# Merging the small-product groups of a chunked gated recurrence: twelve groups a chunk become six, in shared PSUM banks

## The chip, the cores and the metric

The kernel runs on one core of a Trainium2 chip. The metric is the device time of one execution in microseconds (us). All arithmetic is fp32; the large products are made of three passes over split operands.

## The reference, cut to what matters

The program is a decoder layer: projections, a gated linear recurrence (HGRN2), sliding-window attention, two layer norms and a mixture of experts. The change touches the recurrence alone. For each of 4 heads, with keys, queries and decays of width 128, it computes scores that decay from token s to token t:

```python
b = jnp.cumsum(lb_c, axis=2)
diff = b[:, :, :, None, :] - b[:, :, None, :, :]
decay = jnp.exp(jnp.where(tri[:, :, None], diff, -jnp.inf))
scores = jnp.einsum('bhtk,bhtsk,bhsk->bhts', qb, decay, kb)
o_intra = jnp.einsum('bhts,bhsv->bhtv', scores, vb)
...
new_state = (jnp.exp(b_last[:, :, 0, :])[..., None] * state
             + jnp.einsum('bhsk,bhsv->bhkv', kb * jnp.exp(b_last - b), vb))
```

## The kernel before

The program runs in stages: projections with attention, projections with the recurrence, mixing and routing, and the experts. This text is about the second, the recurrence stage (`hgrn`, L520 to L684, and the stage's call at L1450 to L1453).

**The recurrence.** The 1024 tokens are handled as 8 chunks n of 128. For each chunk five tiles are loaded (`load`, L540: `hl` the log decays, `hk`, `hq`, `hv`, `hg`). The 128x128 score matrix of each head is not computed at once, since the decay between two tokens doesn't factor over a whole chunk. It is put together from a diagonal part (`diag`) and seven levels h = 1, 2, 4, ... 64 (`level`): at level h, each pair of neighbouring blocks of h tokens gives one block of scores, and for that level the decay factors over the reference token between the two blocks. `prep_level` (L563) makes the factors of a level in one tile `hE` (two exponentials on ACT at L573 and L576; on DVE a subtraction L575, two multiplications L577 and L580, and the addition L581 that turns `hl` into the running sum that the next level needs).

**The products of a level.** For the diagonal and the levels 1 to 16, `blocks` (L548) makes four products a head, one for each run of 32 tokens: 128 rows deep, 32 columns of weights, 32 moving columns, written to the 32x32 block on the diagonal of the head's 128x128 area in a PSUM bank (`pb`). Four heads make 16 products a group, each two passes in fp32, and the profile shows a pass as one matmul. Of each 32x32 block only the entries that belong to the level count, so `keep` (L535) copies them under a mask into the score tile `hst`, one DVE instruction for each run of 32 partitions. Level 32 makes 8 products (L591, L592), level 64 makes 4 of 64 columns (L589); ACT copies these (L596 to L599).

**The rest of a chunk.** `decay` transposes the decayed keys (L620) for the state; `output` (L643, L645) multiplies scores with values and queries with the last state; its result is squared on ACT (L647), summed on DVE (L649), turned into a norm on POOL (L690) and applied on DVE (L653); `state` (L629, L635) makes the new state; `out` transposes and stores the result (L414).

**The order.** The twelve groups of a chunk get due numbers (L659 to L672), and all groups are sorted by them. When group i is issued, the preparation of group i + 2 is issued first (`group`, L679). `weave` (L231) puts the groups into a stream of filler: the branch-gate projections, 768 matmuls of 512 columns (L103 to L105, three passes `xh*wh`, `xl*wh`, `xh*wl` for each product), spread evenly over the groups. PE issues in this written order; the other engines' instructions are ordered by a scheduler. Filler weights come in as `wr` (L187), and are split into `wh` on ACT (L98) and `wl` on DVE (L99). Filler results leave PSUM through ACT (L508) and DVE (L509).

**Buffers.** `hE` and the chunk's other tiles come out of one set of 24 SBUF tiles; weights, inputs and their splits come out of another set, `q4`, of 36 tiles of twice that size. The `pb` banks are 5, the filler's `mm` banks 3. The loads of the next stage (`mixing_start`) are put in as groups counted from the end (L1451).

Of the kernel before, what the change touches and what calls it, by code (L numbers as in the profile page):

```python
# [5 lines left out]
F32 = mybir.dt.float32  # L6
# [19 lines left out]
RUNS = [slice(b, b + 32) for b in range(0, 128, 32)]  # L26
LEVELS = (64, 32, 16, 8, 4, 2, 1)
# [34 lines left out]
class Builder:  # L62
# [457 lines left out]
    def hgrn(self):  # L520
# [3 lines left out]
        nc = self.nc  # L524
        mm = nc.tensor.matmul
        V = {}
# [4 lines left out]
        def mask(name):  # L531
            m = self.c("ident") if name == 0 else lev[:, WHERE[f"lev{name}"][0] - lo:WHERE[f"lev{name}"][1] - lo]
            return m.bitcast(I32)

        def keep(st, name, pp):  # L535
            for b in RUNS:
                m = mask(name)[b, b][:, None, :].to_broadcast([32, 4, 32])
                nc.vector.copy_predicated(st[b, :, b], m, pp[b, :, b])

        def load(n):  # L540
            t0 = slice(n * 128, n * 128 + 128)
            for nm, src in (("hl", self.hl[:, :, t0]), ("hk", self.hk[:, :, t0]), ("hq", self.hq[:, :, t0]),
                            ("hv", self.hv[t0].rearrange("p (h k) -> p h k", h=4)),
                            ("hg", self.hg[t0].rearrange("p (h k) -> p h k", h=4))):
                V[nm, n] = self.tile([128, 4, 128], F32, nm, 2)
                nc.sync.dma_start(V[nm, n], src)

        def blocks(out, l, r):  # L548

            for b in RUNS:  # L550
                mm(out[b, b], l[:, b], r[:, b], start=True, stop=True)

        def prep_diag(n):
            V["st", n] = self.tile([128, 4, 128], F32, "hst", 1)
            nc.gpsimd.memset(V["st", n], 0.0)

        def diag(n):
            pp = self.bank("pb", (128, 4, 128))
            for hd in range(4):
                blocks(pp[:, hd], V["hk", n][:, hd], V["hq", n][:, hd])  # L560
            keep(V["st", n], 0, pp)

        def prep_level(n, h):  # L563
            q, kT, b = V["hq", n], V["hk", n], V["hl", n]
            ns = 4 * (64 // h)

            def view(t):
                return t.rearrange("p h (s two x) -> p (h s) two x", two=2, x=h)

            e = self.tile([128, 4, 128], F32, "hE", 2)  # L570
            ev, bv, qv, kv = view(e), view(b), view(q), view(kT)
            ref = bv[:, :, 0, h - 1:h].to_broadcast([128, ns, h])
            nc.scalar.activation(ev[:, :, 1], bv[:, :, 1], AF.Exp)  # L573
            if h > 1:
                nc.vector.tensor_sub(ev[:, :, 0], ref, bv[:, :, 0])  # L575
                nc.scalar.activation(ev[:, :, 0], ev[:, :, 0], AF.Exp)  # L576
                nc.vector.tensor_mul(ev[:, :, 0], ev[:, :, 0], kv[:, :, 0])  # L577
            else:
                nc.gpsimd.tensor_copy(ev[:, :, 0], kv[:, :, 0])
            nc.vector.tensor_mul(ev[:, :, 1], ev[:, :, 1], qv[:, :, 1])  # L580
            nc.vector.tensor_add(bv[:, :, 1], bv[:, :, 1], ref)  # L581
            V["e", n, h] = e

        def level(n, h):
            e, st = V.pop(("e", n, h)), V["st", n]
            pp = self.bank("pb", (128, 4, 128))
            for hd in range(4):
                if h == 64:
                    mm(pp[0:64, hd, 64:128], e[:, hd, 0:64], e[:, hd, 64:128], start=True, stop=True)  # L589
                elif h == 32:  # L590
                    mm(pp[0:32, hd, 32:64], e[:, hd, 0:32], e[:, hd, 32:64], start=True, stop=True)  # L591
                    mm(pp[64:96, hd, 96:128], e[:, hd, 64:96], e[:, hd, 96:128], start=True, stop=True)  # L592
                else:
                    blocks(pp[:, hd], e[:, hd], e[:, hd])
            if h == 64:
                nc.scalar.copy(st[0:64, :, 64:128], pp[0:64, :, 64:128])  # L596
            elif h == 32:
                nc.scalar.copy(st[0:32, :, 32:64], pp[0:32, :, 32:64])
                nc.scalar.copy(st[64:96, :, 96:128], pp[64:96, :, 96:128])  # L599
            else:  # L600
                keep(st, h, pp)

        def prep_decay(n):
            b = V["hl", n]
            kdT = self.tile([128, 4, 128], F32, "hkT", 1)
            for hd in range(4):
                nc.scalar.activation(kdT[:, hd], b[:, hd], AF.Exp, scale=-1.0, bias=b[:, hd, 127:128])
            nc.vector.tensor_mul(kdT, kdT, V["hk", n])
            qb = self.tile([128, 4, 128], F32, "hqb", 1)
            nc.scalar.activation(qb, b, AF.Exp)  # L610
            ebl = self.tile([128, 4], F32, "hebl", 2)
            nc.gpsimd.tensor_copy(ebl, qb[:, :, 127])
            nc.vector.tensor_mul(qb, qb, V["hq", n])
            V["d", n] = kdT, qb, ebl

        def decay(n):
            kdT, _, _ = V["d", n]
            kp = self.bank("pb", (128, 4, 128))
            for hd in range(4):
                nc.tensor.transpose(kp[:, hd], kdT[:, hd], self.c("ident"))  # L620
            kd = self.tile([128, 4, 128], F32, "hkd", 1)
            nc.scalar.copy(kd, kp)
            V["kd", n] = kd
# [32 lines left out]
        def out(n):  # L656
            self.out_T(V.pop(("o", n)).rearrange("p h d -> p (h d)"), self.oad, n, "pb")

        none = lambda: None  # L659
        groups = []  # L660
        for n in range(8):
            at = 11 * n
            groups.append((at, lambda n=n: prep_diag(n), lambda n=n: diag(n)))
            for i, h in enumerate(reversed(LEVELS)):
                pre = lambda n=n, h=h: prep_level(n, h)
                if i == 3 and n < 7:
                    pre = lambda n=n, h=h: (load(n + 1), prep_level(n, h))
                groups.append((at + 1 + i, pre, lambda n=n, h=h: level(n, h)))
            groups.append((at + 8, lambda n=n: prep_decay(n), lambda n=n: decay(n)))
            groups.append((at + 10.5, none, lambda n=n: state(n)))  # L670
            groups.append((at + 9.6, none, lambda n=n: output(n)))
            groups.append((at + 13.5, none, lambda n=n: out(n)))  # L672
        groups.sort(key=lambda t: t[0])
        load(0)
        ahead = 2
# [758 lines left out]
    def build(self):  # L1434
        pool = self.tc.tile_pool
        with pool(name="base", bufs=1) as self.base, pool(name="dr", bufs=1, space=DRAM) as self.dr:
            self.setup()
            self.n2 = 13
            self.banks = {"mm": 3, "sc": 1, "pa": 3}
            with pool(name="sb1", bufs=1, reuse_waits="tile") as self.sb, \  # L1440
                    pool(name="ps1", bufs=1, space=PSUM, reuse_waits="tile") as self.ps, self.pe_order():
                self.att_proj()
                self.hg_consts()
                stream = self.stream()
                self.weave(self.attention(), stream, 164)
            self.n2 = 24
            self.banks = {"mm": 3, "pb": 5}
            with pool(name="sb2", bufs=1, reuse_waits="tile") as self.sb, \
                    pool(name="ps2", bufs=1, space=PSUM, reuse_waits="tile") as self.ps, self.pe_order():
                groups = self.hgrn()  # L1450
                for n, fn in zip((16, 11, 7), self.mixing_start()):  # L1451
                    groups.insert(len(groups) - n, fn)
                self.weave(groups, stream, 164, 8)  # L1453
            self.n2 = 4
            with pool(name="sb3", bufs=1, reuse_waits="tile") as self.sb:
                self.banks = {"mm": 4, "pa": 1, "tb": 1, "pb": 2}
                with pool(name="ps3", bufs=1, space=PSUM, reuse_waits="tile") as self.ps:
                    with self.all_order():
                        self.mixing()
                        self.slots()  # L1460
                    self.overflow()
                self.banks = {"mm": 4, "pb": 4}
                with pool(name="ps4", bufs=1, space=PSUM, reuse_waits="tile") as self.ps, self.all_order():
                    self.moe()
# [44 lines left out]
```

## Time and profile before

| | |
|---|---|
| runs of the kernel before, us | 1413.33, 1416.44, 2682.26 (median 1416.44) |
| the profiled execution, us | 1413.68 |
| its span, us | 1411.5 |
| mean granted TensorE clock | 0.985 |
| PE busy in the span | 1347.8 us (95%) |
| DVE busy | 1083.8 us (77%) |
| ACT busy | 790.0 us (56%) |
| recurrence stage | 297.5 to 546 us of the span |

The span is the time from the first to the last instruction in the trace; 2.2 us lie around it. Busy time of PE counts overlapping matmuls once, so what a group costs is read from the starts of the matmuls around it, not from its busy time. Rows name engine, source line, operation, output<-input, and the number of equal instructions.

### The profile page before, as it was taken

The page shows a single profiled execution, that of the slowest core. Times are in us where ns is not written, and L with a number is a line of the kernel's source. Part 1 is how long each engine was busy: PE and PEld are TensorE (multiplying, and loading weights), DVE is VectorE, ACT ScalarE, POOL GpSimd, SP SyncE. Part 2 cuts the span into 40 slices and gives each one's busy share as a digit, 9 for nine tenths or more (in the row PEclk, how much of TensorE's full clock was granted, in tenths as well). Part 3 has the DMA queues.
Part 4 walks back from the last instruction along what each step waited for, and adds up shares of the span by engine and source line. Part 5 has one row for each costly group of instructions (what it writes and reads, how often), then busy time and mean ns, then how long its engine had stood idle before and what let it go on. Part 6 is the DMA issues. An engine that isn't in the chain of part 4 may idle for free. (4 is left out here: it accounts for less than half of the span.)

```text
span 1411.5 us, 22907 instructions
## 1 busy us (share of the span) xinstructions
PE 1347.8 (95%) x8314; PEld 1099.6 (78%) x8314; DVE 1083.8 (77%) x1798; ACT 790.0 (56%) x1282; POOL 243.3 (17%) x160
## 2 busy tenths in 40 slices
PE   7999999999999999999998999999999999999844
PEld 5888899987777778788787788888888888888721
DVE  4268986878778885767746889999999999999645
ACT  4367545424444443312101888888888888888532
POOL 0001212210010001310001122222222222222123
PEclk9999999999999999999999999999999999999967
DMA  6124233253334234865538899999999999999962
GB/s 244 59 88 149 87 112 102 72 175 106 119 129 150 84 105 144 271 194 164 203 135 330 308 364 371 366 356 359 353 350 356 356 357 361 364 365 359 370 259 96
DMA packets 142564, 327.84 MB, mean 232 GB/s; under 512 B 18614, under 2 KB 59702, under 8 KB 142448
## 3 DMA queue, kind: packets, MB, share of 16 engines
q1 hardware_dynamic: 132800, 308.78, 60.3%
q0 software_dynamic: 9648, 17.57, 4.9%
q8 instruction: 66, 1.08, 0.3%
q14 instruction: 50, 0.41, 0.1%
HBM read 291.43 MB, written 52.43 MB: 244 GB/s over the span
## 5 line engine op out<-in xcount | busy, mean ns | idle before, releaser
L99 DVE TENSOR_TENSOR el<-er,eh 128x1024 fp32r<-128x1024 f32 x368 | 436.6, 1220 | 51.9 <-ACT eh L98 34.9
L98 ACT CAST eh<-er 128x1024 fp32r<-128x1024 f32 x368 | 368.7, 1052 | 99.1 <-PE mm L104 82.9
L103 PE MATMUL mm<-xh,wh 128*128 128x512 f32 x480 | 200.2, 417 | 7.8 <-ACT wh L98 6.8
L103 PE MATMUL mm<-eh,xh 128*128 128x512 f32 x496 | 196.4, 396 | 0.0
L104 PE MATMUL mm<-el,xh 128*128 128x512 f32 x496 | 196.2, 395 | 0.0
L105 PE MATMUL mm<-eh,xl 128*128 128x512 f32 x496 | 196.1, 395 | 0.0
L104 PE MATMUL mm<-xl,wh 128*128 128x512 f32 x480 | 189.6, 395 | 0.8 <-DVE xl L99 0.8
L105 PE MATMUL mm<-xh,wl 128*128 128x512 f32 x480 | 190.0, 396 | 0.0
L103 PEld LDWEIGHTS mm<-xh,wh 128*128 128x128 f32 x480 | 91.3, 190 | 26.0 <-ACT wh L98 6.8
L105 PEld LDWEIGHTS mm<-eh,xl 128*128 128x128 f32 x496 | 93.2, 188 | 22.6
L104 PEld LDWEIGHTS mm<-el,xh 128*128 128x128 f32 x496 | 93.2, 188 | 22.3
L103 PEld LDWEIGHTS mm<-eh,xh 128*128 128x128 f32 x496 | 93.2, 188 | 22.3
L105 PEld LDWEIGHTS mm<-xh,wl 128*128 128x128 f32 x480 | 91.2, 190 | 21.1 <-DVE wl L99 0.8
L1075 POOL DMA_INDIRECT xg<-x1d,gi x32 | 58.1, 1816 | 279.7 <-PE pb L1138 245.4
L104 PEld LDWEIGHTS mm<-xl,wh 128*128 128x128 f32 x480 | 91.5, 191 | 16.4 <-DVE xl L99 1.1
L103 PE MATMUL mm<-eh,hth 128*128 128x512 f32 x240 | 100.2, 418 | 0.0
L1079 POOL DMA_INDIRECT zd<-y,gi x29 | 70.4, 2429 | 156.9 <-ACT y L1229 156.9
L105 PE MATMUL mm<-eh,htl 128*128 128x512 f32 x240 | 94.8, 395 | 0.0
L104 PE MATMUL mm<-el,hth 128*128 128x512 f32 x240 | 94.8, 395 | 0.0
L103 PE MATMUL mm<-wh,xh 128*128 128x256 f32 x256 | 73.1, 285 | 0.0
L105 PE MATMUL mm<-wh,xl 128*128 128x256 f32 x256 | 72.4, 283 | 0.0
L104 PE MATMUL mm<-wl,xh 128*128 128x256 f32 x256 | 72.4, 283 | 0.0
(257 smaller groups left out, 2527.4 us busy)
## 6 DMA issues: line engine op xcount, KB each, us to landing
er<-w_g SPq DMA_DIRECT2D x128, 512.0 KB, 12.1
er<-w_u SPq DMA_DIRECT2D x128, 512.0 KB, 12.5
er<-w_d SPq DMA_DIRECT2D x128, 512.0 KB, 12.0
wr<-w_in SPq DMA_DIRECT2D x38, 512.0 KB, 3.8
gated<-st SPq DMA_DIRECT2D x32, 256.0 KB, 2.1
st<-gated SPq DMA_DIRECT2D x32, 256.0 KB, 3.3
xr<-xt SPq DMA_DIRECT2D x8, 512.0 KB, 9.1
wab<-w_a SPq DMA_DIRECT2D x16, 256.0 KB, 3.9
```

The lines of the kernel that those rows point to most:

```text
L98: self.nc.scalar.copy(hi, src)
L99: (eng or self.nc.vector).tensor_sub(lo, src, hi.bitcast(F32))
L103: mm(out, lh, rh, start=start, stop=False)
L104: mm(out, lh, rl, start=False, stop=False)
L105: mm(out, ll, rh, start=False, stop=stop)
L1075: self.nc.gpsimd.indirect_dma_start(to, None, rows, bass.IndirectOffsetOnAxis(ap=self.column(self.gi, e), axis=0), bounds_check=T - 1, oob ...
L1079: self.nc.gpsimd.indirect_dma_start(self.zd, bass.IndirectOffsetOnAxis(ap=idx, axis=0), y, None, bounds_check=T - 1, oob_is_err=False, com ...
```

## The change

The diagonal and the levels 1 and 2 become one group, the levels 4 and 8 another, 16 and 32 a third, 64 and the transposes of the decay a fourth, output and state a fifth; `out` stays alone. In a merged group all products are issued first, one level behind the other, and the copies out of PSUM (now returned as functions) behind all of them. The levels of one group share one bank: each 32x32 block is written at its rows' run shifted by 0, 1 or 2 runs of columns (`RUNS[(i + shift) % 4]`), and `keep` reads it from there. The number of products and of copies stays the same. The two levels' factors lie in one `q4` tile of two halves instead of two smaller tiles. The preparation still runs two groups ahead, and a group is now up to two levels. The due numbers and the places of the next stage's loads are rewritten to match.

```diff
-        def keep(st, name, pp):
-            for b in RUNS:
+        def keep(st, name, pp, shift):
+            for i, b in enumerate(RUNS):
                 m = mask(name)[b, b][:, None, :].to_broadcast([32, 4, 32])
-                nc.vector.copy_predicated(st[b, :, b], m, pp[b, :, b])
+                nc.vector.copy_predicated(st[b, :, b], m, pp[b, :, RUNS[(i + shift) % 4]])
...
-        def blocks(out, l, r):
-
-            for b in RUNS:
-                mm(out[b, b], l[:, b], r[:, b], start=True, stop=True)
+        def blocks(out, l, r, shift):
+
+            for i, b in enumerate(RUNS):
+                mm(out[b, RUNS[(i + shift) % 4]], l[:, b], r[:, b], start=True, stop=True)
...
-        def diag(n):
-            pp = self.bank("pb", (128, 4, 128))
+        def diag(n, pp):
             for hd in range(4):
-                blocks(pp[:, hd], V["hk", n][:, hd], V["hq", n][:, hd])
-            keep(V["st", n], 0, pp)
+                blocks(pp[:, hd], V["hk", n][:, hd], V["hq", n][:, hd], 2)
+            return lambda: keep(V["st", n], 0, pp, 2)
...
-            e = self.tile([128, 4, 128], F32, "hE", 2)
...
-                    blocks(pp[:, hd], e[:, hd], e[:, hd])
...
+                    blocks(pp[:, hd], e[:, hd], e[:, hd], shift)
+
+            def post():
...
+                    keep(st, h, pp, shift)
+
+            return post
+
+        def prep_levels(n, hs):
+            t = self.q4([128, 2, 512], F32, "hE")
+            es = [t[:, j].rearrange("p (h x) -> p h x", h=4) for j in range(2)]
+            for h, e in zip(hs, es):
+                prep_level(n, h, e)
+
+        def levels(n, hs):
+
+            pp = self.bank("pb", (128, 4, 128))
+            posts = [diag(n, pp)] if hs[0] == 1 else []
+            posts += [level(n, h, pp, j) for j, h in enumerate(hs)]
+            for post in posts:
+                post()
...
-            at = 11 * n
...
+            at = 4 * n
+            groups += [(at, lambda n=n: (prep_diag(n), prep_levels(n, (1, 2))), lambda n=n: levels(n, (1, 2))),
+                       (at + 1, lambda n=n: prep_levels(n, (4, 8)), lambda n=n: levels(n, (4, 8))),
+                       (at + 2, lambda n=n: (n < 7 and load(n + 1), prep_levels(n, (16, 32))), lambda n=n: levels(n, (16, 32))),
+                       (at + 3, lambda n=n: (prep_levels(n, (64,)), prep_decay(n)), lambda n=n: (levels(n, (64,)), decay(n))),
+                       (at + 4.5, none, lambda n=n: (output(n), state(n))),
+                       (at + 5.5, none, lambda n=n: out(n))]
...
-                for n, fn in zip((16, 11, 7), self.mixing_start()):
+                for n, fn in zip((8, 6, 4), self.mixing_start()):
```

In the change the lines of `hgrn` move: the subtraction is L573, the multiplications L575 and L578, the addition L579, the decay's products on DVE L623 and L628, the norm's sum L664, its scale L700 and its use L668, the state L650.

PE at the first chunk's first groups (`hq,hk` are the diagonal's operands, `hE` a level's, `mm` the filler), before:

```order
L551 MATMUL pb<-hq,hk 32x32 x16
L103 MATMUL mm<-xh,wh 128x512
L104 MATMUL mm<-xl,wh 128x512
L105 MATMUL mm<-xh,wl 128x512
L103 MATMUL mm<-xh,wh 128x512
L104 MATMUL mm<-xl,wh 128x512
L105 MATMUL mm<-xh,wl 128x512
L551 MATMUL pb<-hE 32x32 x16
```

and in the change:

```order
L105 MATMUL mm<-xh,wl 128x512
L551 MATMUL pb<-hq,hk 32x32 x16
L551 MATMUL pb<-hE 32x32 x32
L103 MATMUL mm<-xh,wh 128x512
L104 MATMUL mm<-xl,wh 128x512
L105 MATMUL mm<-xh,wl 128x512
L103 MATMUL mm<-xh,wh 128x512
```

The levels 1 and 2 (32 products) follow the diagonal's 16 with no filler between; the filler that stood there stands behind the group, 15 matmuls of it before the next group instead of 6 to 9.

DVE between one chunk's output and the next chunk's first copies, in a middle chunk (`const` is the diagonal's mask, `lev` a level's), before:

```order
L653 SCALAR_TENSOR_TENSOR ho<-pb,hss,hg 128x128 x4
L580 TENSOR_TENSOR hE<-hE,hq 128x256
L581 TENSOR_TENSOR hl<-hl 128x256
L635 SCALAR_TENSOR_TENSOR hS<-hS,hebl,pb 128x128 x4
L509 TENSOR_SCALAR st_4601<-st_4601 128x512
L575 TENSOR_TENSOR hE<-hl 128x128x2
L580 TENSOR_TENSOR hE<-hE,hq 128x128x2
L581 TENSOR_TENSOR hl<-hl 128x128x2
L577 TENSOR_TENSOR hE<-hE,hk 128x128x2
L538 COPY_PREDICATED hst<-const,pb 32x4x32 x4
L538 COPY_PREDICATED hst<-lev,pb 32x4x32 x4
```

and in the change:

```order
L538 COPY_PREDICATED hst<-const,pb 32x4x32 x4
L538 COPY_PREDICATED hst<-lev,pb 32x4x32 x8
L575 TENSOR_TENSOR hE<-hE,hk 128x4x64
L579 TENSOR_TENSOR hl<-hl 128x4x64
L664 TENSOR_REDUCE hss<-hsq 128x4
L700 TENSOR_SCALAR hss<-hss 128x4
L668 SCALAR_TENSOR_TENSOR ho<-pb,hss,hg 128x128 x4
L650 SCALAR_TENSOR_TENSOR hS<-hS,hebl,pb 128x128 x4
L509 TENSOR_SCALAR st_4274<-st_4274 128x512
L538 COPY_PREDICATED hst<-lev,pb 32x4x32 x8
```

The copies of the diagonal and of one level alternated with a level's preparation; now twelve copies of the first group stand in a row, ahead of the norm of the chunk before, and eight of the second group behind it.

SP's queue at the start of the stage (`wr` are filler weights, `hl` to `hg` the first chunk's loads, `hgd` a store of the gates), before:

```order
L187 DMA wr_3830<-w_in 128x1024
L187 DMA wr_3832<-w_in 128x1024
L529 DMA lev<-const 128x640
L500 DMA hgd<-st_3040 128x2x256
L546 DMA hl<-hld 128x4x128
L546 DMA hk<-hkd 128x4x128
L546 DMA hq<-hqd 128x4x128
```

and in the change:

```order
L546 DMA hl<-hld 128x4x128
L546 DMA hk<-hkd 128x4x128
L500 DMA hgd<-st_3040 128x2x256
L546 DMA hq<-hqd 128x4x128
L546 DMA hv<-hvd 128x512
L546 DMA hg<-hgd 128x512
```

The two weight loads in front are gone from here (they and the following ones stand behind the loads of the second chunk), and the first two of the chunk's loads have moved ahead of the store.

## Rows read from the trace of the kernel before

**Rows 1.** Windows: busy time of each engine in the stage (count), granted clock, DMA.

```profile
core 0: us, PE busy (x) PEld busy (x) DVE busy (x) ACT busy (x) POOL busy (x), PEclk, DMA share, GB/s
297.50:546.00 248.50, 244.95 (x2747) 189.61 (x2745) 193.20 (x541) 107.83 (x240) 20.43 (x31) 1.00 0.38 121
```

**Rows 2.** Waits of PE in the stage: us in total, times, longest.

```profile
PE pb L589 <- DVE hE L577: 1.1, 2, 0.7
PE pb L620 <- DVE hkT L608: 1.0, 2, 0.8
```

**Rows 3.** Timeline of PE, level 1 of chunk 0: start, us, instruction.

```profile
308.59 0.40 PE L105 MATMUL mm<-xh,wl 128*128 128x512 f32 x1
308.92 0.46 PE L551 MATMUL pb<-hE 128*32 128x32 f32 x32
309.31 0.50 PE L103 MATMUL mm<-xh,wh 128*128 128x512 f32 x1
309.65 0.39 PE L104 MATMUL mm<-xl,wh 128*128 128x512 f32 x1
...
311.26 0.39 PE L105 MATMUL mm<-xh,wl 128*128 128x512 f32 x1
```

**Rows 4.** Timeline of PE, level 32 of chunk 0.

```profile
320.56 0.39 PE L105 MATMUL mm<-xh,wl 128*128 128x512 f32 x1
320.88 0.22 PE L591 MATMUL pb<-hE 128*32 128x32 f32 x1
...
321.13 0.20 PE L592 MATMUL pb<-hE 128*32 128x32 f32 x1
...
321.59 0.39 PE L104 MATMUL mm<-xl,wh 128*128 128x512 f32 x1
```

**Rows 5.** Timeline of PE, level 64 and the decay's transposes of chunk 3.

```profile
411.34 0.68 PE L589 MATMUL pb<-hE 128*64 128x64 f32 x8
...
413.21 0.40 PE L105 MATMUL mm<-xh,wl 128*128 128x512 f32 x1
413.51 0.63 PE L620 MATMUL pb<-const,hkT 128*128 128x128 f32 x4
413.89 0.48 PE L103 MATMUL mm<-xh,wh 128*128 128x512 f32 x1
414.20 0.40 PE L104 MATMUL mm<-xl,wh 128*128 128x512 f32 x1
```

**Rows 6.** Groups of DVE in the stage: count | busy, mean ns | idle before.

```profile
L538 DVE COPY_PREDICATED hst<-lev,pb 32x128 f32<-32x128 int32 x160 | 47.7, 298 | 4.9
L99 DVE TENSOR_TENSOR wl<-wr,wh 128x1024 fp32r<-128x1024 f32 x9 | 11.0, 1224 | 5.3 <-ACT wh L98 3.8 <-PE mm L104 1.5
L653 DVE SCALAR_TENSOR_TENSOR ho<-pb,hss,hg 128x128 f32<-128x128 f32 x32 | 9.0, 343 | 9.0 <-POOL hss L690 9.0
L649 DVE TENSOR_REDUCE hss<-hsq 128x4 f32<-128x512 f32 x8 | 5.5, 685 | 18.0 <-ACT hsq L647 18.0
```

**Rows 7.** Timeline of DVE, one level's preparation in chunk 3.

```profile
405.64 0.42 DVE L575 TENSOR_TENSOR hE<-hl 128x256 f32<-128x256 f32 x1
405.99 0.42 DVE L580 TENSOR_TENSOR hE<-hE,hq 128x256 f32<-128x256 f32 x1
406.32 0.42 DVE L581 TENSOR_TENSOR hl<-hl 128x256 f32<-128x256 f32 x1
406.66 0.42 DVE L577 TENSOR_TENSOR hE<-hE,hk 128x256 f32<-128x256 f32 x1
```

**Rows 8.** Timelines of SP's queue and of PE at the stage's start.

```profile
300.47 0.38 SPq L500 DMA_DIRECT2D hgd<-st  x1
300.90 0.61 SPq L546 DMA_DIRECT2D hl<-hld  x1
...
302.30 0.58 SPq L546 DMA_DIRECT2D hq<-hqd  x1
...
306.94 0.46 PE L551 MATMUL pb<-hq,hk 128*32 128x32 f32 x32 [0.25 <-issue]
```

More of the change, by code (lines that the diff above doesn't have):

```diff
@@ L546, in load, with prep_level @@
                 nc.sync.dma_start(V[nm, n], src)
-        def blocks(out, l, r):
-            for b in RUNS:
-                mm(out[b, b], l[:, b], r[:, b], start=True, stop=True)
+        def blocks(out, l, r, shift):
+            for i, b in enumerate(RUNS):
+                mm(out[b, RUNS[(i + shift) % 4]], l[:, b], r[:, b], start=True, stop=True)
         def prep_diag(n):
-            V["st", n] = self.tile([128, 4, 128], F32, "hst", 1)
+            V["st", n] = self.tile([128, 4, 128], F32, "hst", 2)
             nc.gpsimd.memset(V["st", n], 0.0)
-        def diag(n):
-            pp = self.bank("pb", (128, 4, 128))
+        def diag(n, pp):
             for hd in range(4):
-                blocks(pp[:, hd], V["hk", n][:, hd], V["hq", n][:, hd])
-            keep(V["st", n], 0, pp)
-        def prep_level(n, h):
+                blocks(pp[:, hd], V["hk", n][:, hd], V["hq", n][:, hd], 2)
+            return lambda: keep(V["st", n], 0, pp, 2)
+        def prep_level(n, h, e):
             q, kT, b = V["hq", n], V["hk", n], V["hl", n]
@@ L582, in prep_level, with level @@
             V["e", n, h] = e
-        def level(n, h):
+        def level(n, h, pp, shift):
             e, st = V.pop(("e", n, h)), V["st", n]
-            pp = self.bank("pb", (128, 4, 128))
             for hd in range(4):
@@ L593, in level @@
                 else:
-                    blocks(pp[:, hd], e[:, hd], e[:, hd])
[L595 to L601, printed above, removed]
+                    blocks(pp[:, hd], e[:, hd], e[:, hd], shift)
+            def post():
+                if h == 64:
+                    nc.scalar.copy(st[0:64, :, 64:128], pp[0:64, :, 64:128])
+                elif h == 32:
+                    nc.scalar.copy(st[0:32, :, 32:64], pp[0:32, :, 32:64])
+                    nc.scalar.copy(st[64:96, :, 96:128], pp[64:96, :, 96:128])
+                else:
+                    keep(st, h, pp, shift)
[11 more added lines that the diff above has]
+                post()
         def prep_decay(n):
@@ L661, in hgrn @@
         for n in range(8):
-            at = 11 * n
[L663 to L672, printed above, removed]
+            at = 4 * n
[5 more added lines that the diff above has]
+                       (at + 5.5, none, lambda n=n: out(n))]
         groups.sort(key=lambda t: t[0])
```

## The prediction

> **What bounds the kernel now.** First the windows of the recurrence stage: of its 248.50 us PE is busy in 244.95, at a granted clock of 1.00, while DVE is busy in 193.20 and ACT in 107.83 [rows 1]. So PE sets the length of this stage; only 3.55 us in it are without a matmul. Then the waits of PE: most of that is two waits each for a level's factors and for the decayed keys, both by DVE [rows 2]. ACT and the DMA engines (a share of 0.38) are far from a bound. Last the timeline of PE, since busy time doesn't tell what a small group costs: the starts of the filler matmuls around it do.
>
> What the reader is to see there: filler matmuls start every 0.23 us (from 309.65 to 311.26 in seven steps). From the last filler start ahead of a level group to the second one behind it pass 309.65 - 308.59 = 1.06 us, where two steps of filler alone would be 0.46. So the group costs 0.60 us [rows 3]. But its 32 passes don't need that: the row of 32 lasts 0.46 us in all, and the last of them lasts 0.20 as a single pass does [rows 4], so the starts spread over 0.26 us, 8.4 ns from pass to pass. 32 passes are 0.27 us of work, and 0.33 us are paid once a group: the first pass starts 0.33 after the filler's start instead of 0.23, and the filler behind it is late twice. Level 32 has 16 passes on two of the four column blocks, 16.7 ns apart (320.88 to 321.13 in 15 steps): it costs 321.59 - 320.56 - 0.46 = 0.57 us, of which 16 x 16.7 ns = 0.27 are work and 0.30 are fixed [rows 4]. The decay's transposes work in the filler's own shape; what is fixed there is the step behind them, 0.31 instead of 0.23 [rows 5].
>
> **The change part by part.** *Joins.* Each join of two groups saves one fixed part, and adds no pass. Per chunk: the diagonal with 1, that with 2, and 4 with 8 are three joins at 0.33; 16 with 32 is one at 0.30; level 64 with the transposes, and output with state, save one late step each, 0.08. Sum 0.99 + 0.30 + 0.16 = 1.45 us, times 8 chunks = 11.6 us of PE time. No cover hides or eats this: PE is the stage's bound, and what comes behind the stage (mixing, experts) keeps its order on every engine and moves forward with it.
>
> The trace has no burst of 96 small passes, so the price is bounded from two sides. Low: the passes of the joined part go no faster than level 32's 16.7 ns instead of 8.4 [rows 4]; a join then saves 0.33 - 0.27 = 0.06, and a chunk 0.18 + 0.30 + 0.16 = 0.64, in all 5.1 us. High: the joins with transposes and state save a whole fixed part too, 5 x 0.33 + 0.30 = 1.95 a chunk, 15.6 us. I take 11.6, since it comes from groups of the same shape.
>
> The fixed part stands, in the rows, where 128x32 products follow 128x128 filler and the reverse [rows 3], and a smaller one of 0.08 stands behind transposes of the filler's own shape [rows 5]. The Trainium skill (TensorEngine Tiling (Array Packing), Tiling Modes) says that a change of the tiling mode, not of the tile, drains the engine. By that rule the joins of equal mode save theirs, while 64 columns to 128 and output to state would save nothing: 1.29 a chunk, 10.3 us instead of 11.6. The 0.08 behind the transposes speaks against reading it so strictly.
>
> *Shifted columns and shared banks.* The same passes write the same number of columns, so I put the shift at nothing. The copies are the same 192 instructions of 0.30 us (160 of them, under the levels' masks, in [rows 6]). They start later: the diagonal's copies wait for the whole first group, 0.54 us more. Behind the waiting copy DVE holds the next preparation; that is cheap, because the preparation which PE asks for next was issued two groups, now up to four levels, ahead.
>
> *DVE.* It now has to do in about 236 us what it did in 248.5, and a little more: nine splits of filler weights lie in the stage now [rows 6], and all twelve will (six columns, two halves), since `hE` takes `q4` tiles and the weight loads come later. 193.2 + 3 x 1.22 = 196.9 us. With the waits that nothing covers in the old order, 9.0 for POOL's norm and 18.0 for ACT's square [rows 6], it is 223.9, 28.0 us a chunk against 29.5 of PE. It fits, with 1.5 us to spare. A level takes four steps of about 0.34 us with no gap, copies between them or not [rows 7]: the exponentials are hidden behind the two multiplications and the addition, so taking the copies out from between exposes nothing.
>
> *Margins in a middle chunk.* Preparation of the next chunk's first group stands behind the eight copies of (4, 8): 8 x 0.33 (0.30 busy and the idle time between, 52.6 us for 160 [rows 6]) + 2 x 0.7 (the decay's products, twice the elements of a step of 0.34) + 7 x 0.34 [rows 7] = 6.4 us of work, from the time that PE has done (4, 8). PE asks for it after four stretches of about 15 filler matmuls (3.45 us each) with `out`, (16, 32) and (64, decay) between, some 16 us later. The norm of a chunk (square, sum, POOL, scale) is asked for by `out` two groups later. No new wait here.
>
> *The start.* The first group now needs level 2 at once, and (64, decay) comes earlier. The loads help: `hl` leaves ahead of the last store, and `hq` right behind it, some 1.4 us sooner (302.30 now, with the store at 300.47 and PE waiting 0.25 us for it at 306.94) [rows 8]. `hq` would land near 305.5. From then DVE has, ahead of the decayed keys, 21 steps of preparation (7.1 us), 17 copies (5.6), two splits (2.4) and two scalings (0.7, by the step of [rows 7]): 321.3, and 0.7 for the keys, 322.0. PE gets there at 306.7 + 1.1 + 0.9 + 0.9 (the three level groups) + 0.7 (level 64 [rows 5]) + 3 x 3.45 (filler) = 320.7. So it waits 1.3 us. Carried on through chunk 1 the same count leaves 0.8 us ahead of the first `out` and 0.6 ahead of the second transposes, none later. I put 2.7 us of waits in place of today's 3.55; the bounds are 0 and about 8 (as many in two further chunks).
>
> *The sum.* PE time 244.95 - 11.6 + 2.7 = 236.05 in place of 248.5: 12.45 us less. Against the profiled execution's 1413.68 us (span 1411.5) that is 1401.2, called 1401. The median of the three runs shown is 1416.44, 0.2% above the profiled execution. Against either the gain is 0.9%, below the 2% that a measurement of this kernel can tell from no change.
>
> **Rivals.** *The gain is given back at the start.* DVE's in-order bursts make PE wait in the first chunks for 8 us more than I count. For it: today's waits are all for DVE [rows 2]. Against: each wait there gives the later groups time. 1401 + 8 = 1409.
>
> *The burst is slower than its parts.* Passes of a long burst go at 16.7 ns: gain 5.1 + 0.85, time 1407.7. For it only that level 32 shows such a pace; against it, that level has half the column blocks. If nothing at all were saved by joining, the time would stay at 1413.
>
> *Slower: DVE becomes the clock of the stage.* Its need is 28.0 us a chunk by the sum above, the stage has 31.06 today. If the bursts of twelve and eight copies add 4 us of waiting a chunk (each burst starts only when its whole group is done, and the preparation behind it then runs into the next burst), a chunk takes 32.0: 1413.7 + 8 x 0.94 = 1421. It decides from 3.1 us a chunk on. For it: DVE's 78% of the stage and the late norm; against: 16 us of margin. The Trainium skill (TensorEngine Tiling (Array Packing), PSUM Bottleneck) warns that tiling speeds up TensorE but not the evacuation of PSUM, which may become the limit; in this trace evacuation on DVE is 57 us of 248.5, so the rule alone doesn't reach it.
>
> *More than forecast.* All waits go and the joins save 15.6: 1413.7 - 15.6 - 3.55 = 1394.5.
>
> **How the numbers follow.** Forecast (1397 to 1405) 0.62; given back at the start 0.13; slow burst 0.10; DVE as clock 0.06; more than forecast 0.06; nothing saved 0.03. The range 1396 to 1413 holds the forecast and the two cases that return part of it. A gain over 2% (below 1385) would need more than the high bound: 0.02. A loss over 2% (above 1442) needs 34.6 us a chunk of DVE, or a stage that I haven't seen: 0.03. Within 2%: 0.95.
>
> **What would show it.** The stage's window from the first filler of the gates to mixing should be about 236 us. On PE a group of 96 passes should last about 1.0 us, and cost about 1.1 by the filler's starts; a group of 64 about 0.87. A longer one makes the slow burst right. Waits of PE for `hkT` and `ho` should stand in chunks 0 and 1 alone, 2 to 3 us in all. DVE's wait for the square should shrink; if DVE shows no idle time ahead of the norm and PE waits in every chunk, DVE is the clock. The forecast is wrong if the stage shrinks by under 5 us, or if a later stage changes by more than 2.

## The result, and the profile after

The changed kernel takes 1399.93 us (median of 4 runs, 1399.77 to 1401.49); 1401 was predicted, 1396 to 1413 the range. The ratio to the kernel before is 0.9895, with a 95% interval of 0.9882 to 0.9909; it is taken without the one run of 2682.26 us of the kernel before. The profiled execution took 1399.95 us, its span 1398.2.

First the recurrence stage. The windows of the kernel after, over the whole stage and over four middle chunks (columns as in [rows 1]):

```profile
core 0: us, PE busy (x) PEld busy (x) DVE busy (x) ACT busy (x) POOL busy (x), PEclk, DMA share, GB/s
297.50:535.00 237.50, 234.89 (x2751) 191.28 (x2750) 199.10 (x547) 111.15 (x246) 18.31 (x32) 1.00 0.43 137
375.40:482.30 106.90, 106.90 (x1336) 87.69 (x1335) 97.68 (x276) 53.62 (x124) 8.14 (x16) 1.00 0.43 137
```

The first row answers to [rows 1]: PE still bounds the stage, and the stage is shorter. From its first filler to the first matmul of mixing it was 546.04 - 297.66 = 248.38 us, and is 532.93 - 296.83 = 236.10: 12.28 less (predicted 236.05). What lies behind the stage is the same (865.46 us before, 865.27 after). The stage begins 0.83 us earlier in the span, which the change doesn't explain. In the second row PE has no gap at all in four chunks of 26.7 us, and DVE is busy in 91% of them.

PE's timeline at the first two groups of chunk 0 answers to [rows 3]:

```profile
305.47 0.39 PE L105 MATMUL mm<-xh,wl 128*128 128x512 f32 x1
305.79 0.46 PE L551 MATMUL pb<-hq,hk 128*32 128x32 f32 x32
306.06 0.76 PE L551 MATMUL pb<-hE 128*32 128x32 f32 x64
306.75 0.51 PE L103 MATMUL mm<-xh,wh 128*128 128x512 f32 x1
307.09 0.39 PE L104 MATMUL mm<-xl,wh 128*128 128x512 f32 x1
...
310.04 0.39 PE L105 MATMUL mm<-xh,wl 128*128 128x512 f32 x1
310.36 0.76 PE L551 MATMUL pb<-hE 128*32 128x32 f32 x64
311.05 0.51 PE L103 MATMUL mm<-xh,wh 128*128 128x512 f32 x1
311.39 0.39 PE L104 MATMUL mm<-xl,wh 128*128 128x512 f32 x1
```

Read as in the prediction: from the filler start ahead (305.47) to the second behind (307.09) is 1.62 us, less 0.46 for two filler steps: the diagonal with levels 1 and 2 costs 1.16 us, where three groups cost 0.58 + 0.59 + 0.59. Levels 4 and 8 cost 311.39 - 310.04 - 0.46 = 0.89. The step into the narrow products (0.32) and the step behind them (0.34 in place of 0.23) are paid once.

The medians over all chunks, before and after: diagonal, 1, 2: 1.76 to 1.16; levels 4, 8: 1.18 to 0.895; 16, 32: 1.165 to 0.84; 64 and decay: 1.26 to 1.20; output and state: 2.70 to 2.69. The joins save 0.60 + 0.285 + 0.325 + 0.06 + 0.01 = 1.28 us a chunk, 10.2 us in all.

What PE waited for inside the stage, in answer to [rows 2]:

```profile
engine line waited for: us in total, times, longest us
PE pb L414 <- DVE ho L668: 1.5, 1, 1.5
PE mm L103 <- ACT st L508: 0.7, 1, 0.7
PE pb L635 <- DVE hkT L623: 0.4, 1, 0.4
```

The waits for `hE` are gone. By the starts around the groups, waits are somewhat longer than these rows: the decay's transposes cost 0.47 us more than usual in chunk 0 and 0.08 in chunk 1, the transposes of the result 0.51 and 2.15. Together 3.2 us, all in chunks 0 and 1; before it was 3.8 by the same count. The largest is in chunk 1. On DVE, and then PE:

```profile
363.24 0.42 DVE L575 TENSOR_TENSOR hE<-hE,hk 128x256 f32<-128x256 f32 x1
363.58 0.68 DVE L664 TENSOR_REDUCE hss<-hsq 128x4 f32<-128x512 f32 x1
364.29 0.17 DVE L700 TENSOR_SCALAR hss<-hss 128x4 f32<-128x4 f32 x1
365.59 1.12 DVE L668 SCALAR_TENSOR_TENSOR ho<-pb,hss,hg 128x128 f32<-128x128 f32 x4 [1.13 <-POOL hss L701]
...
366.00 1.10 PE L414 MATMUL pb<-const,ho 128*128 128x128 f32 x4 [1.50 <-DVE ho L668]
```

DVE reaches the norm only at 363.58, behind preparation and copies; PE's last filler had started at 364.11.

The groups of DVE that answer to [rows 6]:

```profile
L99 DVE TENSOR_TENSOR wl<-wr,wh 128x1024 fp32r<-128x1024 f32 x14 | 16.8, 1222 | 0.7 <-ACT wh L98 0.7
L668 DVE SCALAR_TENSOR_TENSOR ho<-pb,hss,hg 128x128 f32<-128x128 f32 x32 | 9.0, 344 | 9.4 <-POOL hss L701 8.2 <-PE mm L104 1.2
L664 DVE TENSOR_REDUCE hss<-hsq 128x4 f32<-128x512 f32 x8 | 5.5, 681 | 7.0 <-ACT hsq L662 7.0
```

Fourteen weight splits lie in this window, and DVE's wait for the square fell from 18.0 to 7.0 us, all of it at one place.

So the 12.28 us of the stage are 10.2 of joins and 0.6 of waits; the other 1.5 lie in the filler, whose mean step, without the first behind each group, fell from 0.2299 to 0.2277 us (671 such steps after).

### The profile page after: what moved, and what is told of

Its sections match the earlier page's. It is cut to its first block, busy times and chain, and to the rows that moved or that the text cites. A ratio compares the mean times of both kernels' runs of the same rounds, so it can differ in the third digit from the quotient of the medians.

```text
span 1398.2 us, 22818 instructions
## 1 busy us (share of the span) xinstructions
PE 1335.6 (96%) x8314; PEld 1100.5 (79%) x8314; DVE 1080.5 (77%) x1798; ACT 789.4 (56%) x1282; POOL 241.8 (17%) x160
## 3 DMA queue, kind: packets, MB, share of 16 engines
q1 hardware_dynamic: 132800, 308.78, 60.9%
## 5 line engine op out<-in xcount | busy, mean ns | idle before, releaser
L103 PE MATMUL mm<-xh,wh 128*128 128x512 f32 x480 | 194.9, 406 | 7.8 <-ACT wh L98 6.8
L1086 POOL DMA_INDIRECT xg<-x1d,gi x32 | 58.1, 1816 | 279.3 <-PE pb L1149 255.4
```

The costliest lines, as they stand in the source:

```text
L103: mm(out, lh, rh, start=start, stop=False)
L1086: self.nc.gpsimd.indirect_dma_start(to, None, rows, bass.IndirectOffsetOnAxis(ap=self.column(self.gi, e), axis=0), bounds_check=T - 1, oob ...
```

## The experiments

The theory: each switch of PE from 128x512 filler to narrow products and back costs a fixed part of about 0.3 us, and the gain is the fixed parts that the joins remove. The rivals: it comes from preparation that runs further ahead; the shared bank and its shift bring or cost something. A second question came up on the way: why two chunks still wait, and how far joining can go.

Start and tail of the program vary by up to 3 us among kernels whose code there is the same (the stage begins at 294.6 to 297.7, and 865.2 to 868.5 us lie behind it). The comparison therefore also goes by the stage, with two counts from PE's timeline in it: what all groups cost by the filler starts around them, waits included; and what filler steps at half clock (0.43 us in place of 0.23) cost more. Ratios are to the kernel before on the same chip. Only E7 differs from it by more than 2%, and stage, groups and half clock come from one profiled execution of each kernel.

| kernel | median, us | ratio, 95% interval | stage, us | groups, us | half clock, us |
|---|---|---|---|---|---|
| before | 1415.69 | | 248.38 | 71.8 | 0 |
| the change | 1399.93 | 0.9895 (0.9882, 0.9909) | 236.10 | 60.9 | 0 |
| E1 unjoined | 1408.65 | 0.9960 (0.9946, 0.9974) | 244.96 | 67.9 | 0 |
| E2 joins only | 1401.59 | 0.9918 (0.9890, 0.9947) | 238.51 | 62.7 | 0 |
| E3 own banks | 1401.06 | 0.9907 (0.9890, 0.9925) | 236.32 | 60.5 | 0 |
| E4 cut | 1428.81 | 1.0103 (1.0086, 1.0121) | 262.50 | 85.5 | 0 |
| E5 late result | 1402.12 | 0.9922 (0.9904, 0.9940) | 237.84 | 61.1 | 1.6 |
| E6 two groups | 1409.28 | 0.9969 (0.9959, 0.9979) | 245.65 | 67.3 | 3.6 |
| E7 one group | 1460.05 | 1.0336 (1.0315, 1.0356) | 294.22 | 107.6 | 12.2 |
| E8 late start | 1397.64 | 0.9889 (0.9868, 0.9911) | 233.32 | 58.1 | 0 |
| E9 both late | 1402.91 | 0.9922 (0.9900, 0.9943) | 238.56 | 63.3 | 0 |
| E10 three groups | 1399.53 | 0.9895 (0.9873, 0.9917) | 236.23 | 60.3 | 1.0 |
| E11 and GpSimd | 1395.69 | 0.9885 (0.9859, 0.9910) | 232.57 | 57.3 | 0 |
| E12 early result | 1400.16 | 0.9903 (0.9887, 0.9920) | 238.47 | 61.6 | 1.5 |

**E1, the joins undone on PE alone.** A merged group hands back its parts, and filler is woven between them.

```diff
-            for post in posts:
-                post()
...
+            return parts[:-1] + [last]
...
-        return [lambda i=i: group(i) for i in range(len(groups))]
...
+        return [lambda i=i, k=k: group(i, k) for i in range(len(groups)) for k in range(groups[i][3])]
```

> The changed kernel with the joins undone on TensorE alone: preparation two merged groups ahead, shared banks, shifts and buffers stay, but filler lies again between the parts of a group. If the joins make the gain (a fixed part of about 0.3 us saved at each of three joins of 32 columns and at 16 with 32, nearly nothing at the decay and the state), 1.28 us a chunk come back: 10.2 us, about 1410, with single groups of 32 passes costing 0.58 to 0.60 again. If the gain lies in the preparation that runs further ahead and in the waits, the time stays at 1400 to 1402.

Single groups cost 0.58 to 0.59 again, and nothing waits inside a group. The groups cost 67.9 us against 60.9: 10.2 of joins come back and 3.2 of waits go (+7.0). The time is 8.7 us above the change. So the preparation further ahead doesn't make this gain. It isn't worth nothing, though: against the kernel before, E1 is faster as well (0.9960, the interval below 1). Its stage is 3.4 us shorter with the same number of groups, because the 3.8 us of waits there are gone. Something besides the joins takes these waits away: the preparation further ahead, the loads' places, the buffers or the order. No run took these apart, and with the joins 3.2 us of waits are back.

**E2, the kernel before with the joins alone.** Groups are issued back to back, with preparation five groups ahead; state, output and result get later due numbers. Banks, columns and factor tiles stay as before.

```diff
-        ahead = 2
+        ahead = 5
...
-        return [lambda i=i: group(i) for i in range(len(groups))]
...
+        return [lambda ix=ix: [group(i) for i in ix] for ix in order]
```

> The kernel before with the joins alone: groups are issued back to back as in the change, but each level keeps its own bank, unshifted, its own factor tile of the old pool and its own preparation step (five levels ahead). If the joins make the gain: 1400 to 1403, groups of 96 passes costing about 1.16 us. If the shared bank or the merged preparation is needed for it: 1408 to 1415, with waits of TensorE inside the groups.

The joins pay the same here: 0.885, 0.845, 1.19 and 2.69 us for the last four groups. The first group costs 1.295 at the median, with waits of its own in chunks 0 and 1:

```profile
PE pb L551 <- DVE hE L577: 1.9, 2, 1.4
PE pb L551 <- DMA hq<-hqd: 0.6, 1, 0.6
```

So neither the shared bank nor the merged preparation is needed for most of the gain. The stage is 2.4 us longer than in the change, 1.8 of it in the groups, mostly by the waits at the start.

**E3, the change with a bank for each level.**

```diff
-            pp = self.bank("pb", (128, 4, 128))
-            posts = [diag(n, pp)] if hs[0] == 1 else []
-            posts += [level(n, h, pp, j) for j, h in enumerate(hs)]
+            bank = lambda: self.bank("pb", (128, 4, 128))
+            posts = [diag(n, bank())] if hs[0] == 1 else []
+            posts += [level(n, h, bank(), 0) for h in hs]
```

> The changed kernel with a bank for each level and no shift; joins, order, preparation and buffers stay. If shift and sharing cost and bring nothing: 1400, within 1.5 us, and a group of 96 passes still costs about 1.16 us. If the passes of two levels to one bank hinder each other, 2 to 8 us less; if the shared bank saves waits for free banks, 2 us more or above.

The stage is 0.2 us longer than in the change, a group of 96 passes costs 1.18, one of 64 passes 0.89. Sharing and shifting cost nothing that can be measured and bring nothing; they spare banks.

**E4, the opposite of a join.** Each 16-product group of the kernel before is cut in two, with filler between.

```diff
-            for hd in range(4):
+            for hd in (0, 1) if part == 0 else (2, 3):
```

> The kernel before with each of its six groups of 16 products a chunk cut in two by filler: the same passes, 48 more switches between 128x512 filler and 128x32 products. If a fixed part of 0.33 us hangs on each switch there and back: 48 x 0.33 = 15.8 us more, about 1430, and each half of 16 passes costs 0.33 + 0.13 = 0.46 us. If the fixed part belongs to a group's start (its wait, its new bank), a cut costs at most 0.1 us and the time is below 1419.

PE's timeline at the first halves of level 1:

```profile
307.00 0.40 PE L105 MATMUL mm<-xh,wl 128*128 128x512 f32 x1
307.33 0.33 PE L551 MATMUL pb<-hE 128*32 128x32 f32 x16
307.59 0.50 PE L103 MATMUL mm<-xh,wh 128*128 128x512 f32 x1
307.93 0.39 PE L104 MATMUL mm<-xl,wh 128*128 128x512 f32 x1
```

A half costs 307.93 - 307.00 - 0.46 = 0.47 us (median 0.46, as expected), and two halves 0.92 where the whole cost 0.59: 0.33 us a switch, in each of 48. The fixed part hangs on the switch, not on what the group waits for. The stage grew by 14.1 us: 15.8 less about 2 of waits that the finer weave takes away.

**E5, the result's transposes one group later.** They waited most in the change, so they were moved.

```diff
-                       (at + 5.5, none, lambda n=n: out(n))]
+                       (at + 6.5, none, lambda n=n: out(n))]
```

> The changed kernel with the transposes of a chunk's result issued one group later. If TensorE's waits for the result in chunks 0 and 1 (0.5 and 2.15 us above the usual 0.45 of a group) are DVE's lateness at the start, which the later chunks make good, they go: about 2.6 us less, 1397.5, and the group costs 0.45 in all chunks. If DVE is short throughout, the wait moves to the next group that needs DVE (level 4 of the next chunk or the decayed keys), and the time stays at 1399 to 1401.

Neither answer came out whole: their cost is 0.45 in every chunk, but the wait moved to levels 16 and 32 of chunk 1, and something came on top. PE there:

```profile
334.44 0.39 PE L105 MATMUL mm<-xh,wl 128*128 128x512 f32 x1
335.95 0.46 PE L551 MATMUL pb<-hE 128*32 128x32 f32 x32 [1.12 <-DVE hE L575]
337.88 0.22 PE L588 MATMUL pb<-hE 128*32 128x32 f32 x1 [1.48 <-DVE hE L575]
...
338.26 0.63 PE L103 MATMUL mm<-xh,wh 128*128 128x512 f32 x1
338.69 0.63 PE L104 MATMUL mm<-xl,wh 128*128 128x512 f32 x1
339.12 0.63 PE L105 MATMUL mm<-xh,wl 128*128 128x512 f32 x1
```

Behind two waits close together the filler starts every 0.43 us, eight times, and then again every 0.23. The window over that stretch shows why (clock in the column behind POOL's):

```profile
338.50:342.00 3.50, 3.50 (x9) 2.70 (x9) 3.25 (x12) 0.42 (x1) 0.00 (x0) 0.52 0.20 75
```

The granted clock is 0.52, the lower of its two levels (1.2 GHz), for about 3.5 us, which cost 1.6 us on top of the waits. In the change PE waited 1.50 us once, and the clock stayed at 1.00.

**E8, the first group 18 filler matmuls (4.1 us) later.**

```diff
-                self.weave(groups, stream, 164, 8)
+                self.weave(groups, stream, 164, 12)
```

> The changed kernel with its first group 19 filler matmuls (4.3 us) later, the others spread over what is left (each gap 3% shorter). If the waits of chunks 0 and 1 (0.5, 0.5, 0.1 and 2.15 us above the groups' usual cost) are a backlog of VectorE from the stage's start, most of them go: about 1397. If VectorE is short throughout (its slack ahead of the result's transposes is only 0.6 to 2.1 us in chunks 2 to 5), the shorter gaps bring waits there: 1400 or more.

One wait of 0.45 us is left in the groups (58.1 us against 60.9), and the stage is 2.8 us shorter. So the waits of chunks 0 and 1 are a backlog at the start. The time is 1397.64; its interval doesn't part it from the change.

**E9, both.**

```diff
-                       (at + 5.5, none, lambda n=n: out(n))]
+                       (at + 6.5, none, lambda n=n: out(n))]
...
-                self.weave(groups, stream, 164, 8)
+                self.weave(groups, stream, 164, 12)
```

> The changed kernel with both: the first group 4.3 us later and the result's transposes one group later. With the late transposes alone TensorE waited 1.12 and 1.48 us at levels 16 and 32 of chunk 1, and eight filler matmuls behind went at 0.43 us, a granted clock of 0.52. If the later start clears VectorE's backlog, no wait is left, the clock stays at 1.00 and the time is 1396 to 1398. If not, a wait of over 2 us and a stretch at half clock remain: 1400 to 1403.

PE waited 3.0 us for the result of chunk 3. The cause stands on SP and ACT:

```profile
410.95 0.53 SPq L546 DMA_DIRECT2D hl<-hld  x1
...
417.43 0.44 ACT L571 ACTIVATE hE<-hl 128x256 f32<-128x256 f32 x1 [4.48 <-DMA hl<-hld]
...
419.36 0.57 ACT L662 ACTIVATE hsq<-pb 128x512 f32<-128x512 f32 x1
```

This `hl` is chunk 5's. ACT waits 4.48 us for it, DVE with it, and the square of chunk 3's result (L662) stands behind that wait, so the norm comes late. In the change the square stands ahead of the wait for the same `hl`:

```profile
412.25 0.60 ACT L662 ACTIVATE hsq<-pb 128x512 f32<-128x512 f32 x1 [0.71 <-PE pb L660]
...
419.94 0.45 ACT L571 ACTIVATE hE<-hl 128x256 f32<-128x256 f32 x1 [2.79 <-DMA hl<-hld]
```

E8 has the order of the change, E5 that of E9, so the late result brings it. By itself it did no harm to this result: in E5 ACT waited 4.49 us at the same place, but started on `hl` 3.6 us after its issue, in E9 6.5 us after. Why that load took longer in E9 no run shows. A due number moved not only PE's instruction, but the order of another engine's work.

**E6, two more joins a chunk.** Diagonal, 1, 2, 4 in one bank; 8, 16, 32 in another, with 64 and the decay.

```diff
-                       (at + 1, lambda n=n: prep_levels(n, (4, 8)), lambda n=n: levels(n, (4, 8))),
...
+            groups += [(at, lambda n=n: (prep_diag(n), prep_levels(n, (1, 2)), prep_levels(n, (4,))), lambda n=n: levels(n, (1, 2, 4))),
...
+                        lambda n=n: (levels(n, (8, 16, 32, 64)), decay(n))),
```

> The changed kernel with two more joins a chunk: diagonal, 1, 2 and 4 in one bank (four shifts), then 8, 16, 32 in one bank with 64 (a bank of its own) and the decay's transposes behind. By the join theory two more fixed parts of about 0.31 us go in each of 8 chunks: 5.0 us less than the change, about 1395; the group of 128 passes should cost 0.33 + 4 x 0.28 = 1.44 us, the second group 0.9 + 0.84 + 1.2 less two fixed parts. The rival, DVE: bursts of 16 and 12 copies and preparation four levels at a time make TensorE wait in every chunk: 1400 or more, with rows of waits on hE, hkT or ho in later chunks.

The first group costs 1.43, the second 2.12 where nothing waits: 3.55 a chunk against 4.10, 4.4 us saved in all, as the theory has it. But PE's waits in the stage are:

```profile
PE pb L636 <- DVE hst L538: 8.3, 4, 3.9
PE pb L414 <- DVE ho L669: 2.7, 3, 1.7
PE pb L659 <- ACT hst L598: 1.3, 1, 1.3
```

and behind the longest of them the clock falls:

```profile
339.44 1.09 PE L636 MATMUL pb<-const,hkT 128*128 128x128 f32 x4 [3.86 <-DVE hst L538]
...
340.75 0.63 PE L104 MATMUL mm<-xl,wh 128*128 128x512 f32 x1
341.18 0.63 PE L105 MATMUL mm<-xh,wl 128*128 128x512 f32 x1
```

The rival came true: 12.3 us of waits and 3.6 at half clock stand against the joins. The decay's transposes don't read `hst`; what they and the copies share is the banks. By the code's order the transposes ask for the sixth bank, counting the first group's as the first, and there are five, so they wait until DVE's sixteen copies have emptied that one. The trace agrees; the last ten of the sixteen:

```profile
336.05 3.24 DVE L538 COPY_PREDICATED hst<-lev,pb 32x128 f32<-32x128 int32 x10
```

They end at 339.29, and the transposes start at 339.44; their own operand `hkT` was ready at 335.41. No run with a sixth bank tested it.

**E7, one level group a chunk.** A chunk's loads and its whole preparation are now issued together too, and the first group starts later. Against E6:

```diff
-                        lambda n=n: (levels(n, (8, 16, 32, 64)), decay(n))),
+                        lambda n=n: (levels(n, (1, 2, 4)), levels(n, (8, 16, 32, 64)), decay(n))),
```

> All level groups and the decay's transposes of a chunk in one group: one switch a chunk from filler to narrow products and back. By the join theory one more fixed part a chunk than with two groups, 2.5 us less than that kernel: about 1392.5 without new waits. The rival, DVE: 28 copies (9 us) and the whole next preparation (11 us) then stand in a row between two such groups, about 26 us apart; if TensorE waits for the result or the factors in every chunk, 1400 or above.

```profile
PE pb L414 <- DVE ho L669: 32.9, 6, 13.5
PE pb L551 <- issue: 9.9, 4, 3.0
```

PE waits for the result of six chunks, and 12.2 us more are lost at half clock. What the 9.9 us of the second row wait for the profile doesn't show.

**E10, three groups** (diagonal, 1, 2, 4; then 8, 16, 32; then 64 and decay), late start, late result.

```diff
+            groups += [(at, lambda n=n: (prep_diag(n), prep_levels(n, (1, 2)), prep_levels(n, (4,))), lambda n=n: levels(n, (1, 2, 4))),
...
+                       (at + 2, lambda n=n: (prep_levels(n, (64,)), prep_decay(n)), lambda n=n: (levels(n, (64,)), decay(n))),
```

> Three level groups a chunk instead of four (diagonal, 1, 2, 4; then 8, 16, 32; then 64 with the decay), each level group one bank, with the later start and the later result. One more join a chunk, 0.31 us: 2.5 us less than the kernel with both delays if VectorE keeps up, about 1394.5; the groups should cost 1.43, 1.13 and 1.20 us. If VectorE doesn't: waits of TensorE in chunks 2 to 5 and stretches at half clock, 1400 to 1410.

The groups cost 1.43, 1.13 and 1.20 us as expected, 0.33 a chunk less. One wait of 3.11 us for the decayed keys in chunk 6, with four filler steps at half clock behind it, and two small ones give it back: the stage is as long as the change's.

**E11, and the gates' scale on GpSimd.**

```diff
-                nc.vector.tensor_scalar(e, e, 0.5, 0.5, op0=ALU.mult, op1=ALU.add)
+                nc.gpsimd.tensor_scalar(e, e, 0.5, 0.5, op0=ALU.mult, op1=ALU.add)
```

> As the kernel with three level groups, and the scale and shift of the filler's gates (32 instructions of 0.42 us on VectorE, 13.6 us) done on GpSimd. If VectorE's load is what limits further joins, this takes 1.7 us a chunk from it: waits of the kernel with three groups go, about 1394 or that kernel's time less its waits. If VectorE was not the limit, the time equals that kernel's within 1 us; GpSimd's own instruction can be slower (no row shows it) and hold the filler's output tiles: up to 5 us more.

```profile
L509 POOL TENSOR_SCALAR st<-st 128x512 f32<-128x512 f32 x32 | 23.0, 719 | 117.8 <-ACT st L508 110.3 <-DMA gated<-st 6.5 <-DVE hst L538 1.0
```

An instruction takes 0.72 us there instead of 0.42 on DVE, on an engine that was mostly idle. Waits fall from 4.4 to 2.1 us (decayed keys, 1.15 and 0.95, in chunks 1 and 6), the clock stays at 1.00, and the stage is the shortest of all, 232.57. That points to DVE's load as what stops further joins, but it isn't shown by the times: the runs of E10 (1396.90 to 1400.14 us) and of E11 (1394.67 to 1400.12) overlap, and the profiled execution is the slowest of four in E10 and the fastest in E11. At 1395.69 us E11 beats the kernel before; against the change and against E8 the intervals overlap.

**E12, E11 with the result's transposes one group earlier.**

```diff
-                       (at + 5.5, none, lambda n=n: out(n))]
+                       (at + 4.5, none, lambda n=n: out(n))]
```

> As the kernel with three level groups and the gates' scale on GpSimd, but the result's transposes go back one group, to where the change has them relative to output and state. If the late result is what pushed VectorE's work on the decayed keys behind their due time (two waits of 1.15 and 0.95 us, in chunks 1 and 7), the waits go and the time is 1393 to 1395, about 2 us below the kernel with late transposes and 4 below the change with the later start alone. If VectorE has nothing to spare in the three-group order either way, the waits move to the transposes of the result and the time stays at 1395 to 1398.

The waits moved to the transposes of the result (1.40, 0.38, and 2.76 with half clock behind it), the second answer, and the time is worse than expected by it, 1400.16. In both orders of three groups PE waits for DVE, with the scale on GpSimd too.

## Why the prediction was right

*What bounds the kernel, and the joins.* PE bounds the stage, and a join saves the fixed part: E1, E2 and E4 show it by taking the joins away, adding them alone, and doing the opposite. The term was a little large: 1.28 us a chunk instead of 1.45. Of its parts, two joins of 32 passes gave 0.60 instead of 0.66, levels 4 and 8 0.285 instead of 0.33, 16 with 32 0.325 instead of 0.30, the decay 0.06 and the state 0.01 instead of 0.08 each.

The Trainium skill (TensorEngine Tiling (Array Packing), Tiling Modes) says that changing the tiling mode, not just the tile, drains the engine. The state's 0.01 agrees with it: output and state are both 128x128. The decay's 0.06 is close to the nothing that the prediction read out of that rule.

The prediction's sum by the rule was 10.3 us, and the runs show 10.2. That is partly luck, since the joins of equal mode were put at 1.29 a chunk and gave 1.21. The reason given against the rule, a late step of 0.08 behind the transposes, was wrong for the state.

*Waits.* 2.7 us were put, 3.2 are there, in chunks 0 and 1 as said. The sum hid errors: 1.3 ahead of the first decayed keys was 0.47, and 2.15 at the second result was forecast as none; that the total fits is luck. E8 shows that they are a backlog at the start.

*DVE, and the margins.* "It fits" held, by a wrong count. The step divided the stage by eight (29.5 us of PE a chunk); the middle chunks come every 26.7 us, and DVE is busy in 24.4 of them, with some 1.2 of waiting for POOL's norm on top. The split weights were fourteen instead of twelve, which is all of the difference between 199.1 us busy and the forecast 196.9. And "no new wait here" for the norm rested on two groups of distance, without counting what DVE does first: in chunk 2 the result is ready at 391.86 + 1.12 and asked for at 393.60, 0.6 us later; before, it was ready 7.7 us ahead.

```profile
391.86 1.12 DVE L668 SCALAR_TENSOR_TENSOR ho<-pb,hss,hg 128x128 f32<-128x128 f32 x4 [1.19 <-POOL hss L701]
...
393.60 0.60 PE L414 MATMUL pb<-const,ho 128*128 128x128 f32 x4
```

In chunks 3 to 5 the result is 0.9 to 2.1 us ahead. The step failed, and behind chunk 1 it cost nothing only because no later chunk crossed that line: that is luck. Half of the prediction's own sign for DVE as the clock is there: in seven of eight chunks DVE has no idle time ahead of the norm's sum. The other half, waits of PE in every chunk, is not.

*Shift and shared banks* cost nothing (E3). *The sum* of the stage was 236.05 and came out as 236.10 by luck: 1.4 us less in joins was met by some 1.5 in the filler, which was not in the sum. The filler's step goes with the number of groups: its mean is 0.2299 and 0.2307 us in the kernels with 96 groups (before, E1), and 0.2278 to 0.2287 in those with 48 (the change, E2, E3, E8). A small part is the tail of a group: the second to fourth filler steps behind a group take 0.231 us in the kernel before and later ones 0.229, and half as many groups have half as many tails, 0.3 us. The rest is open.

*The rivals.* The slow burst is out: the second and the third 32 passes of a group cost 0.29 us each, not 0.53. DVE as the clock of the stage did not happen with six groups a chunk, but it is the next bound, nearer than the 0.06 made it: in E6, E7, E10 and E12 PE's main waits are for DVE. The Trainium skill (TensorEngine Tiling (Array Packing), PSUM Bottleneck) warns that evacuation may become the limit behind faster tiles. E6's wait of 8.3 us for copies out of `pb` agrees with it; in the change no such wait stands.

## What to carry to other kernels

Where narrow products are woven into wide ones, count the switches: here each to 32-column products and back cost 0.3 us whether 16, 32 or more passes stood in the group, while the joins of the wider products saved next to nothing. The price can be read before any change from the starts of the wide matmuls around one group. Before joining further, measure for each thing that the bounding engine asks for how long ago it was ready, per chunk, in the steady part of the stage; here DVE was busy for 91% with 0.6 us of slack, and the next joins were given back in waits (E6, E10). And moving a due number can move other engines' work past each other (E9), and the use of banks with it.

## What the runs showed of the hardware that was not expected

A wait of PE can cost more than its length. Behind waits of 1.12 and 1.48 us with narrow products between (E5), of 3.86 us (E6) and of 3.11 us (E10), the next four to nine filler matmuls started every 0.43 us instead of 0.23 at a granted clock near 0.5. In E12, behind a wait of 2.76 us, the first three filler steps took 0.31, 0.24 and 0.28 us, and only then seven of 0.43 followed. It is not settled by the length of the last wait alone. In E6 the clock also fell behind a wait of 1.89 us, and not behind one of 1.71. In E9 it stayed at 1.00 behind this one:

```profile
427.43 1.11 PE L414 MATMUL pb<-const,ho 128*128 128x128 f32 x4 [3.01 <-DVE ho L668]
428.29 0.48 PE L103 MATMUL mm<-xh,wh 128*128 128x512 f32 x1
428.61 0.39 PE L104 MATMUL mm<-xl,wh 128*128 128x512 f32 x1
428.84 0.39 PE L105 MATMUL mm<-xh,wl 128*128 128x512 f32 x1
```
